# First stage of a two-layer decoder trunk: constants on another queue, the positions' product and the low parts in another order

## The chip, the cores and the metric

The kernel runs on one core of a Trainium2 chip. The metric is the device time of one launch, in microseconds (us): the median of three runs, and lower is better. A profile was taken of one execution; all rows below are of that execution, with times counted from the start of its span.

TensorE (PE in the rows; its weight loads are PEld) multiplies matrices, VectorE (DVE) and ScalarE (ACT) work element by element, GpSimd (POOL) does little here, and SyncE (SP) issues nearly all DMAs.

## What is computed

The reference is a decoder trunk of two layers over 256 tokens of width 1024. Each layer modulates its input by a conditioning vector, projects it, runs three kinds of attention side by side, and ends in a squared-ReLU MLP. What matters here is the very beginning, the modulation and the input projection of layer 0:

```python
mod = jax.nn.silu(c) @ ada_w[l] + ada_b[l]
sh_a, sc_a, g_a, sh_m, sc_m, g_m = [m_[:, None, :] for m_ in jnp.split(mod, 6, axis=-1)]
h = x * (1 + sc_a) + sh_a
parts = jnp.split(h @ w_in[l], SPLIT_POINTS, axis=-1)
...
ob, _ = banded_attention(rope(bq, positions), rope(bk, positions), bv, B_WINDOW - 1, sinks=sinks[l])
```

`rope` needs the sine and cosine of each position times a frequency.

## The kernel before

Every large product is done in three passes: each float32 operand is split into a high part and a low part, and the kernel adds high by high, high by low and low by high. A split is one ScalarE copy (`whi`, line 189) and one VectorE subtraction (`wlo`, line 191).

The first stage handles the 1024 input channels of layer 0 in eight chunks of 128. For each chunk `kc`:

- `first_h` computes the modulation of the chunk: sixteen small matmuls (line 177, `gv`) of the column form `crep` of silu(c) with a 1 MB block of the conditioning weights (`raw`, from `ada0`), a copy `rs` on ScalarE (line 324), two transposes of `x` (line 327) and a tiny product (line 328) that turns the sums into a column. VectorE adds the bias (`md`, line 330). Then ScalarE writes the high part of the modulated input (`hT`, line 332), VectorE computes the same in full (`h`, line 334) and subtracts to get the low part (`hT`, line 335).
- `first_load` loads the chunk's rows of the projection in two pieces (`w`, 768 and 792 columns, line 345), and `first_chunk` splits both pieces and multiplies: thirty matmuls `mm` of 256 columns (line 357 high by high, line 359 high weights by low input, line 360 low weights by high input) and six `mmv` of 280 columns (lines 402 to 404; 404 reads the low input). Lines 360 and 403 need the low parts of the weights, lines 359 and 404 the low part of `hT`.

The chunk's matmuls don't all stand together: a scheduler puts the end of chunk kc behind the `gv` matmuls and the column form of chunk kc+1, and the order on every engine is fixed when the program is built. `issue_after(X)` asks it to issue what is inside only once X has been issued.

All of this needs `p1`, one small tile (154 columns, 77 KB) that holds c, biases, a selector and the identity matrix. It is loaded by ScalarE's queue (line 138). SyncE's queue begins with the first `raw` block, the first half of `x`, the two pieces of `w`, and the next `raw`. TensorE starts with `WARM` matmuls of the identity by itself (`warm`, line 942), which compute nothing that is used, and has `FILL` more of them while the first `hT` is made.

The rotary tables are a generator, `rope_tables`, in three steps: a product of the positions' row by ones (line 661) with the multiplication by the frequencies (line 662); a chain of VectorE operations that brings the angles into range (lines 665 to 679); and two sines on ScalarE (lines 681 and 682), each of the switches of function costing a table load. `START` says after which chunk a step is taken: `o` is the next step of the tables, `r` the rows of the bias tables, `e` an exponential that switches ScalarE's table back.

Of the kernel before, what the change touches and what calls it, by code (L numbers as in the profile page):

```python
# [10 lines left out]
F32 = mybir.dt.float32  # L11
# [3 lines left out]
OP = mybir.AluOpType  # L15
# [12 lines left out]
SPARES = (('w', 'P', 'qk'), ('w', 'qk', 'P', 'mx'))  # L28
EARLY = 3
FO = (1, 3)  # L30
WARM = 8
TURN = 6
ORDER = ('kv0..21s4.3sa5.s.Acb.6.B7C..Ee', '.ts..q0412...ss3s.kva5cb.67AB.E..Ce')
GV = ('v', 'h', 'v', 'v', 'v')
START = ('', 'or', 'oe', '', '', '', '', '', 'cbbp')
FILL = 3
GROUPS = ((0, 4, 0), (4, 8, 32))


# [84 lines left out]
def trunk_kernel(ctx: ExitStack, tc: tile.TileContext, a):  # L124
    nc = tc.nc
# [9 lines left out]


    p1 = cst.tile([128, NP1], F32, name="p1")
    nc.scalar.dma_start(p1, a["p1"])
    pi32 = att.tile([128, S], I32, name="pi32", tag="pTc", bufs=2)
    nc.gpsimd.dma_start(pi32[0:1], bass.AP(tensor=a["positions"].tensor, offset=a["positions"].offset, ap=[[S, 1], [1, S]]))  # L140
    frs = cst.tile([128, 2], F32, name="frs")
# [165 lines left out]
                    fill.pop(0)  # L307


    SUMS, H32 = [], []  # L310

    def first_h(kc):

        gv = ps.tile([128, 512], F32, name="gv", tag="pt")
        tp = gv[:, 256:512].rearrange("p (b t) -> p b t", b=2)
        t = rawload(a["ada0"][kc])
        if kc % 2 == 0:
            nc.sync.dma_start(x[:, :, kc * 128:kc * 128 + 256], a["x"][:, :, kc * 128:kc * 128 + 256])
        for k in range(KC):
            for s in range(2):  # L320
                j = 2 * (k % 2) + s
                end = gemv_mm(gv, t, k, j, (k * 2 + s) * 128, 128, k < 2, k >= KC - 2)
        rs = u2("rs")
        SUMS.append(nc.scalar.activation(rs[:, :128], gv[:, :128], AF.Copy).ins)
        yield end.ins
        for b in range(2):
            nc.tensor.transpose(tp[:, b], x[:, b, kc * 128:kc * 128 + 128], ident)
        nc.tensor.matmul(gv[:, 128:130], rs[:, :128], p1[:, 24:26], start=True, stop=True)
        md = sm.tile([128, 2], F32, name="md0")
        nc.vector.tensor_tensor(md, gv[:, 128:130], p1[:, 8 + 2 * kc:10 + 2 * kc], op=OP.add)  # L330

        nc.scalar.activation(hT[:, 0, kc], gv[:, 256:512], AF.Identity, bias=md[:, 1:2], scale=md[:, 0:1])
        h32 = u2("h32")[:, :S]
        H32.append(nc.vector.tensor_scalar(h32, gv[:, 256:512], md[:, 0:1], md[:, 1:2], op0=OP.mult, op1=OP.add).ins)
        nc.vector.tensor_tensor(hT[:, 1, kc], h32, hT[:, 0, kc].bitcast(F32), op=OP.subtract)
        yield

    def first_load(kc):
# [9 lines left out]
    def first_chunk(kc, ts, prs, vs):  # L348

        with tc.issue_after(SUMS[kc]):  # L350
            ws = [parts(t, m, behind=H32[kc]) for t, m in ts]
        for pr, o in enumerate(prs):
            hi, lo = ws[pr // 3]
            for i in range(2):
                c = slice((2 * pr % 6 + i) * 128, (2 * pr % 6 + i + 1) * 128)

                nc.tensor.matmul(o[:, i], hi[:, c], hT[:, 0, kc], start=kc == 0 and i == 0, stop=False,
                                 skip_group_check=True)
                nc.tensor.matmul(o[:, i], hi[:, c], hT[:, 1, kc], start=False, stop=False, skip_group_check=True)
                nc.tensor.matmul(o[:, i], lo[:, c], hT[:, 0, kc], start=False, stop=kc == KC - 1,  # L360
                                 skip_group_check=True)
            yield
        hi, lo = (w[:, 512:] for w in ws[1])
        for b, o in enumerate(vs):
            v_mm(o, b, kc, hi, lo)
        yield
# [286 lines left out]
    def rope_tables(o):  # L653

        t = new_P()
        an, k, f, g = (t[:, i] for i in range(4))
        row = u2("row")[0:1]
        nc.vector.memset(row[:, S:S + 128], 1.0)
        with tc.issue_after(crep_set.ins):
            nc.vector.tensor_copy(row[:, :S], pi32[0:1])  # L660
        nc.tensor.matmul(o, row[:, S:S + 128], row[:, :S], start=True, stop=True)
        nc.vector.tensor_scalar(an, o, frs[:, 0:1], None, op0=OP.mult)
        yield
        magic = 1.5 * 2 ** 23
        nc.vector.tensor_scalar(k, an, 1.0 / (2 * math.pi), magic, op0=OP.mult, op1=OP.add)
        nc.vector.tensor_scalar(k, k, magic, None, op0=OP.subtract)
        c1 = 6.28125
        c2 = float(np.round((2 * math.pi - c1) * 2 ** 20) / 2 ** 20)
        c3 = 2 * math.pi - c1 - c2
        for c in (c1, c2, c3):  # L670
            nc.vector.scalar_tensor_tensor(an, k, -c, an, op0=OP.mult, op1=OP.add)

        nc.vector.scalar_tensor_tensor(f, an, -1.0, an, op0=OP.mult, op1=OP.max)
        nc.vector.tensor_scalar(f, f, -1.0, math.pi / 2, op0=OP.mult, op1=OP.add)

        nc.vector.tensor_scalar(k, an, -1.0, math.pi, op0=OP.mult, op1=OP.add)
        nc.vector.tensor_tensor(g, an, k, op=OP.min)
        nc.vector.tensor_scalar(k, an, -1.0, -math.pi, op0=OP.mult, op1=OP.add)
        nc.vector.tensor_tensor(g, g, k, op=OP.max)
        yield  # L680
        nc.scalar.activation(cosT, f, AF.Sin)
        nc.scalar.activation(sinT, g, AF.Sin)
        nc.vector.tensor_scalar(sinT, sinT, frs[:, 1:2], None, op0=OP.mult)
        yield
# [255 lines left out]
    def warm_up(n):  # L940
        for i in range(n):
            nc.tensor.matmul(warm[:, :128], ident, ident, start=True, stop=True)
# [7 lines left out]
    for kc in range(KC + 1):  # L950
        h = first_h(kc) if kc < KC else iter(())
        if kc == 0:
            end = next(h)
            with tc.issue_after(end):
                next(rt)
            w0, _ = first_load(0)
        if kc:
            ch = first_chunk(kc - 1, w0, prs, vs)
            end = next(h, None)
            if kc < KC:  # L960
                w0, loaded = first_load(kc)
            for _ in range(FO[1]):
                next(ch)
            if FO[0] and end:
                with tc.issue_after(end):
                    next(ch)
            next(h, None)
            next(h, None)
            for _ in ch:
                pass  # L970
        else:
            next(h)
            warm_up(FILL)
        for j in START[kc]:
            if j == "o":
                next(rt)
            elif j == "r":
                btab = bias_tables(bias_rows())
            elif j == "e":

                nc.scalar.activation(se[:, 0], sinT[:, 0:KC], AF.Exp)
            else:

                with tc.issue_after(loaded):
                    if j == "c":
                        nc.sync.dma_start(co, a["co"])
                    elif j == "p":
                        nc.sync.dma_start(p2, a["p2"])
                    else:
                        next(btab)  # L990
# [304 lines left out]
```

## Time and profile before

| | |
|---|---|
| median of 3 runs | 697.76 us (697.71 to 699.91) |
| the profiled execution's own time | 696.37 us |
| its span in the trace | 694.6 us |
| TensorE busy | 668.2 us, 96% of the span |
| VectorE busy | 497.6 us, 72% |
| ScalarE busy | 402.6 us, 58% |
| DMA moved | 167.55 MB, mean 241 GB/s |

The span leaves out 1.77 us of the execution's own time. An engine's busy time counts the union of its instructions; TensorE's instructions overlap, so a row's duration is longer than its distance to the next row.

### The profile page before, as it was taken

How to read it: one execution, taken by the hardware profiler on the slowest of the kernel's cores; microseconds unless marked ns; L12 is line 12 of the kernel's file. 1: busy time of each engine (PE TensorE's matmuls, PEld its weight loads, DVE VectorE, ACT ScalarE, POOL GpSimd, SP SyncE). 2: the span in 40 equal slices, each digit the busy share in tenths (PEclk: the TensorE clock that was granted, in tenths of full speed). 3: DMA queues.
4: the chain of work that ended last, by engine and by line, in shares of the span. 5: the costliest groups of instructions: out<-in, count | busy, mean ns of one | idle time of the engine just before them, and what ended most of it. 6: DMA issues, size and time to landing. Idle time of an engine off the chain costs nothing.

```text
span 694.6 us, 11202 instructions
## 1 busy us (share of the span) xinstructions
PE 668.2 (96%) x4302; PEld 550.1 (79%) x4302; DVE 497.6 (72%) x965; ACT 402.6 (58%) x792; POOL 43.1 (6%) x43
## 2 busy tenths in 40 slices
PE   5999999999999999999999999999999999999995
PEld 4888859558888888788889967867898888888884
DVE  3444968958798878888877967657679755555756
ACT  2534474874855555556746356688474655656641
POOL 0000200000400000000013010000130000000004
PEclk9999999999999999999999999999999999999998
DMA  8879788669359899889763958610438965655501
GB/s 324 290 270 351 263 325 277 236 232 345 127 223 365 311 371 341 326 334 341 278 242 122 347 175 309 238 62 1 182 137 290 377 220 189 210 188 186 182 0 62
DMA packets 29474, 167.55 MB, mean 241 GB/s; under 512 B 3247, under 2 KB 6475, under 8 KB 11884
## 3 DMA queue, kind: packets, MB, share of 16 engines
q1 hardware_dynamic: 29148, 166.73, 65.9%
q8 instruction: 34, 0.56, 0.3%
q14 instruction: 20, 0.16, 0.1%
q10 hardware_dynamic: 144, 0.08, 0.1%
q0 software_dynamic: 128, 0.02, 0.0%
HBM read 165.74 MB, written 1.08 MB: 240 GB/s over the span
## 4 chain that ended last, share of the span: by engine, by line
PE 87%; DVE 6%; ACT 4%; issue 1%; DMA 1%; POOL 0%; DVEq 0%; POOLq 0%
PE mm L394 14%; PE mmv L411 8%; PE m L1189 8%; PE m L1190 8%; PE m L1191 8%; PE mm L395 7%; PE s L734 3%; PE tp L702 2%; PE mm L383 2%; PE mm L381 2%; PE mm L382 2%; PE wo L1124 2%; PE wo L1126 2%; PE wo L1125 2%; PE gv L177 2%; PE acc L750 2%
## 5 line engine op out<-in xcount | busy, mean ns | idle before, releaser
L191 DVE TENSOR_TENSOR wlo<-raw,whi 128x1024 fp32r<-128x1024 f32 (+3 forms) x174 | 196.7, 1154 | 49.9 <-ACT whi L189 48.5
L189 ACT ACTIVATE whi<-raw 128x1024 fp32r<-128x1024 f32 (+3 forms) x183 | 178.8, 1003 | 34.9 <-PE mm L394 14.5
L394 PE MATMUL mm<-hT,whi 128*128 128x512 f32 x416 | 148.1, 399 | 0.0
L395 PE MATMUL mm<-hT,wlo 128*128 128x256 f32 x416 | 116.2, 281 | 1.2 <-DVE wlo L191 1.2
L1189 PE MATMUL m<-whi,mx 128*128 128x512 f32 x250 | 97.8, 391 | 0.0
L1190 PE MATMUL m<-wlo,mx 128*128 128x512 f32 x250 | 97.7, 391 | 0.0
L1191 PE MATMUL m<-whi,mx 128*128 128x512 f32 x250 | 97.2, 390 | 0.0
L394 PEld LDWEIGHTS mm<-hT,whi 128*128 128x128 f32 x416 | 78.1, 188 | 20.8 <-issue 2.1
L395 PEld LDWEIGHTS mm<-hT,wlo 128*128 128x128 f32 x416 | 78.5, 189 | 3.4 <-DVE wlo L191 2.3
L255 DVE SCALAR_TENSOR_TENSOR qk<-raw,se,qk 128x1024 f32<-128x1024 f32 x56 | 71.2, 1282 | 0.2
L397 ACT ACTIVATE P<-mm 128x256 f32<-128x256 f32 x52 | 19.7, 379 | 66.0 <-PE mm L395 66.0
L1189 PEld LDWEIGHTS m<-whi,mx 128*128 128x128 f32 x250 | 46.9, 188 | 10.1
L411 PE MATMUL mmv<-whi,hT 128*128 128x256 f32 (+2 forms) x352 | 53.9, 298 | 1.0 <-ACT hT L492 1.0
L1191 PEld LDWEIGHTS m<-whi,mx 128*128 128x128 f32 x250 | 46.9, 188 | 10.0
L1190 PEld LDWEIGHTS m<-wlo,mx 128*128 128x128 f32 x250 | 46.9, 188 | 8.9
L690 ACT ACTIVATE P<-P,sxt 128x128 f32<-128x128 f32 (+1 forms) x96 | 42.8, 448 | 18.2 <-DVE sxt L688 18.0
L411 PEld LDWEIGHTS mmv<-whi,hT 128*128 128x128 f32 x352 | 48.0, 189 | 2.5 <-ACT hT L492 1.5
L446 POOL TENSOR_TENSOR ve<-ve,co 128x1 f32<-128x1 f32 x8 | 4.4, 551 | 543.6 <-DVE ve L445 443.6
L381 PE MATMUL mm<-hT,whi 128*128 128x256 f32 x128 | 37.6, 294 | 0.0
L383 PE MATMUL mm<-hT,wlo 128*128 128x256 f32 x128 | 37.3, 291 | 0.1
L382 PE MATMUL mm<-hT,whi 128*128 128x256 f32 x128 | 36.6, 286 | 0.0
L398 DVE TENSOR_TENSOR P<-P,mm 128x256 f32<-128x256 f32 x52 | 21.7, 417 | 18.6 <-ACT P L397 18.5
(244 smaller groups left out, 1126.6 us busy)
## 6 DMA issues: line engine op xcount, KB each, us to landing
raw<-in_mlp_w_dram SPq DMA_DIRECT2D x64, 1024.0 KB, 6.0
raw<-in_ada_dram SPq DMA_DIRECT2D x32, 1024.0 KB, 5.4
raw<-in_adag_dram SPq DMA_DIRECT2D x16, 1024.0 KB, 6.2
raw<-in_w_in_dram SPq DMA_DIRECT2D x9, 1024.0 KB, 6.9
raw<-in_cmp_w_dram SPq DMA_DIRECT2D x8, 1024.0 KB, 6.8
raw<-in_w_out_dram SPq DMA_DIRECT2D x8, 1024.0 KB, 4.7
w<-in_w_in_dram SPq DMA_DIRECT2D x8, 396.0 KB, 7.2
w<-in_w_in_dram SPq DMA_DIRECT2D x8, 384.0 KB, 3.2
```

What stands on the lines that cost most here:

```text
L189: nc.scalar.activation(hi, t, AF.Copy)
L191: (eng or nc.vector).tensor_tensor(lo, t, hi.bitcast(F32), op=OP.subtract)
L255: nc.vector.scalar_tensor_tensor(ac, src, by, ac, op0=OP.mult, op1=OP.add)
L381: nc.tensor.matmul(o[:, i], hi[:, c], hT[:, 0, kc], start=kc == 0, stop=False, skip_group_check=True)
L382: nc.tensor.matmul(o[:, i], hi[:, c], hT[:, 1, kc], start=False, stop=False, skip_group_check=True)
L383: nc.tensor.matmul(o[:, i], lo[:, c], hT[:, 0, kc], start=False, stop=kc == KC - 1, skip_group_check=True)
L394: nc.tensor.matmul(o, hi[:, c], hT[:, :, kc], start=kc == 0, stop=False, skip_group_check=True)
L395: nc.tensor.matmul(o[:, 0], lo[:, c], hT[:, 0, kc], start=False, stop=kc == KC - 1, skip_group_check=True)
L411: nc.tensor.matmul(o, hT[:, x_, kc, t], ws[kc][w_], start=kc == 0 and x_ + w_ == 0, stop=kc == KC - 1 and w_ == 1)
L1189: nc.tensor.matmul(o, f[:, 0, i, t], hi, start=first, stop=False)
L1190: nc.tensor.matmul(o, f[:, 0, i, t], lo, start=False, stop=False)
L1191: nc.tensor.matmul(o, f[:, 1, i, t], hi, start=False, stop=lastk)
```

## The change

Five edits, all in the first stage:

- `p1` is loaded by SyncE's queue, ahead of everything else on it.
- `rope_tables` has one step more: the cast of the positions into a row stands by itself, and the product with the multiplication by the frequencies comes after VectorE's `md` of chunk 0. The range reduction moves from chunk 1 to chunk 2 and must follow that chunk's `h`; the sines and the exponential move from chunk 2 to chunk 3.
- The low parts of the weights of a chunk are issued after the low part of `hT` (`LOW`), no longer after the full `h` (`H32`).
- `WARM` goes from 8 to 9, `FILL` from 3 to 2.
- The row of the positions is no longer held back behind the last `gv` matmul of chunk 0.

```diff
-WARM = 8
+WARM = 9
...
-START = ('', 'or', 'oe', '', '', '', '', '', 'cbbp')
-FILL = 3
+START = ('', 'r', 'o', 'oe', '', '', '', '', 'cbbp')
+FILL = 2
...
-    nc.scalar.dma_start(p1, a["p1"])
+    nc.sync.dma_start(p1, a["p1"])
...
-        nc.vector.tensor_tensor(md, gv[:, 128:130], p1[:, 8 + 2 * kc:10 + 2 * kc], op=OP.add)
+        MD.append(nc.vector.tensor_tensor(md, gv[:, 128:130], p1[:, 8 + 2 * kc:10 + 2 * kc], op=OP.add).ins)
...
-        nc.vector.tensor_tensor(hT[:, 1, kc], h32, hT[:, 0, kc].bitcast(F32), op=OP.subtract)
+        LOW.append(nc.vector.tensor_tensor(hT[:, 1, kc], h32, hT[:, 0, kc].bitcast(F32), op=OP.subtract).ins)
...
-            ws = [parts(t, m, behind=H32[kc]) for t, m in ts]
+            ws = [parts(t, m, behind=LOW[kc]) for t, m in ts]
...
             nc.vector.tensor_copy(row[:, :S], pi32[0:1])
+        yield
         nc.tensor.matmul(o, row[:, S:S + 128], row[:, :S], start=True, stop=True)
...
-            end = next(h)
-            with tc.issue_after(end):
-                next(rt)
+            next(h)
+            next(rt)
...
             next(h)
+            with tc.issue_after(MD[0]):
+                next(rt)
             warm_up(FILL)
...
-                next(rt)
+                with tc.issue_after(H32[-1]):
+                    next(rt)
```

The orders differ in the first stage and shortly after it; from the first units of attention on they are the same on every engine. Three places matter.

TensorE at the start of the program, as a difference (`warm<-p_78` is the idle matmul, `warm<-row` the positions' product, `gv<-p_78,rs` the column form):

```order
-L942 MATMUL warm<-p_78 128x128 x8
+L943 MATMUL warm<-p_78 128x128 x9
 L177 MATMUL gv<-raw,crep 32x128 x16
 L327 MATMUL gv<-p_78,x 128x128 x2
-L661 MATMUL warm<-row 128x256
 L328 MATMUL gv<-p_78,rs 128x2
-L942 MATMUL warm<-p_78 128x128 x3
+L662 MATMUL warm<-row 128x256
+L943 MATMUL warm<-p_78 128x128 x2
 L357 MATMUL mm<-hT,whi 128x256 x2
```

The positions' product has moved behind the column form. Behind the last row there came two L402 and then L359 before; now there come two L359, one L402, and then L360.

VectorE in chunk 0, before (`P<-warm,frs` is the multiplication by the frequencies, the `P<-P` rows are the range reduction):

```order
L662 TENSOR_SCALAR P<-warm,frs 128x256
L330 TENSOR_TENSOR md_158<-gv,p_78 128x2
L665 TENSOR_SCALAR P<-P 128x256
L666 TENSOR_SCALAR P<-P 128x256
L671 SCALAR_TENSOR_TENSOR P<-P 128x256
L334 TENSOR_SCALAR h_161<-gv,md_158 128x256
L191 TENSOR_TENSOR wlo<-w_151,whi 128x768
L335 TENSOR_TENSOR hT<-h_161,hT 128x256
L191 TENSOR_TENSOR wlo<-w_153,whi 128x792
```

VectorE in chunk 0, after the change:

```order
L330 TENSOR_TENSOR md_157<-gv,p_78 128x2
L663 TENSOR_SCALAR P<-warm,frs 128x256
L334 TENSOR_SCALAR h_160<-gv,md_157 128x256
L335 TENSOR_TENSOR hT<-h_160,hT 128x256
L191 TENSOR_TENSOR wlo<-w_150,whi 128x768
L191 TENSOR_TENSOR wlo<-w_152,whi 128x792
```

The range reduction is gone from here, the frequencies stand behind `md`, and the low part of `hT` stands ahead of both low parts of the weights, as in every later chunk.

TensorE around the column form of chunk 2, before:

```order
L328 MATMUL gv<-p_78,rs 128x2
L359 MATMUL mm<-hT,whi 128x256
L360 MATMUL mm<-hT,wlo 128x256
L357 MATMUL mm<-hT,whi 128x256
L359 MATMUL mm<-hT,whi 128x256
L360 MATMUL mm<-hT,wlo 128x256
L403 MATMUL mmv<-wlo,hT 128x280
L404 MATMUL mmv<-whi,hT 128x280
L403 MATMUL mmv<-wlo,hT 128x280
L404 MATMUL mmv<-whi,hT 128x280
L357 MATMUL mm<-hT,whi 128x256 x4
L402 MATMUL mmv<-whi,hT 128x280 x2
```

TensorE at the same place after the change:

```order
L328 MATMUL gv<-p_78,rs 128x2
L403 MATMUL mmv<-wlo,hT 128x280
L404 MATMUL mmv<-whi,hT 128x280
L402 MATMUL mmv<-whi,hT 128x280
L403 MATMUL mmv<-wlo,hT 128x280
L404 MATMUL mmv<-whi,hT 128x280
L357 MATMUL mm<-hT,whi 128x256 x3
L359 MATMUL mm<-hT,whi 128x256 x3
L357 MATMUL mm<-hT,whi 128x256
L360 MATMUL mm<-hT,wlo 128x256
```

Four matmuls fewer of chunk 1 stand behind the column form, and chunk 2's own begin with three L357, three L359 and soon an L360; before, there came four L357 and two L402, and only then the first L359.

VectorE in the same chunk 2, after the change, has two operations of the range reduction between its own:

```order
L334 TENSOR_SCALAR h_324<-gv,md_321 128x256
L666 TENSOR_SCALAR P<-P 128x256
L335 TENSOR_TENSOR hT<-h_324,hT 128x256
L667 TENSOR_SCALAR P<-P 128x256
L191 TENSOR_TENSOR wlo<-w_282,whi 128x768
L672 SCALAR_TENSOR_TENSOR P<-P 128x256
L191 TENSOR_TENSOR wlo<-w_284,whi 128x792
```

L666 stands ahead of the low part of `hT`, L667 ahead of the first low part of the weights; before, nothing of the range reduction stood in chunk 2.

## Rows read from the trace of the kernel before

**Rows 1.** Whom TensorE waited for, whole span: us in total, times, longest.

```profile
PE warm L942 <- DMA p<-in_p_dram: 6.5, 1, 6.5
PE mm L359 <- DVE hT L335: 2.2, 5, 0.8
...
PE sw L920 <- ACT ct L915: 0.9, 1, 0.9
```

**Rows 2.** The chain that ended last, first 60 us: start, length, what.

```profile
0.74 5.72 DMA p<-in_p_dram
...
18.29 0.12 PE mm L359
```

**Rows 3.** Timeline, chunk 0: start, duration, engine, line, instruction, idle time before.

```profile
0.74 0.39 SPq L145 DMA_DIRECT2D raw<-in_ada_dram  x1
...
1.20 0.66 SPq L318 DMA_DIRECT2D x<-in_x_dram  x1
...
6.50 3.55 PE L942 MATMUL warm<-p 128*128 128x128 f32 x16 [6.50 <-DMA p<-in_p_dram]
...
9.98 1.08 PE L177 MATMUL gv<-raw,crep 128*32 128x128 f32 x32
...
11.83 0.69 PE L661 MATMUL warm<-row 1*128 1x256 f32 x2
...
12.46 0.38 PE L328 MATMUL gv<-p,rs 128*128 128x2 f32 x2
12.56 0.48 DVE L662 TENSOR_SCALAR P<-warm,frs 128x256 f32<-128x256 f32 x1 [4.63 <-PE warm L661]
12.96 0.15 DVE L330 TENSOR_TENSOR md<-gv,p 128x2 f32<-128x2 f32 x1
13.08 0.29 DVE L665 TENSOR_SCALAR P<-P 128x256 f32<-128x256 f32 x1
...
14.54 0.95 DVE L191 TENSOR_TENSOR wlo<-w,whi 128x768 fp32r<-128x768 f32 x1
15.40 0.42 DVE L335 TENSOR_TENSOR hT<-h,hT 128x256 fp32r<-128x256 f32 x1
...
15.87 0.39 PE L359 MATMUL mm<-hT,whi 128*128 128x256 f32 x1 [0.83 <-DVE hT L335]
...
19.07 1.28 ACT L681 ACT_TABLE_LOAD   x1
```

**Rows 4.** Timeline around the column form of chunk 2, in order of time.

```profile
27.10 0.28 PE L328 MATMUL gv<-p,rs 128*128 128x2 f32 x2
...
27.49 0.16 DVE L330 TENSOR_TENSOR md<-gv,p 128x2 f32<-128x2 f32 x1 [2.85 <-PE gv L328]
...
27.68 0.56 ACT L332 ACTIVATE hT<-gv,md 128x256 fp32r<-128x256 f32 x1 [0.72 <-DVE md L330]
...
28.28 0.55 DVE L334 TENSOR_SCALAR h<-gv,md 128x256 f32<-128x256 f32 x1 [0.63 <-ACT hT L332]
...
28.44 1.01 PE L357 MATMUL mm<-hT,whi 128*128 128x256 f32 x4
...
29.28 0.42 PE L402 MATMUL mmv<-whi,hT 128*128 128x280 f32 x2
...
30.08 0.39 PE L359 MATMUL mm<-hT,whi 128*128 128x256 f32 x1 [0.39 <-DVE hT L335]
```

**Rows 5.** Profile page, DMA issues: queue, count, KB each, median us to landing.

```profile
w<-in_w_in_dram SPq DMA_DIRECT2D x8, 384.0 KB, 3.2
```

**Rows 6.** Engines and DMA in two stretches; granted clock, DMA share, GB/s stand last.

```profile
2.00:3.00 1.00, 0.00 (x0) 0.00 (x0) 0.00 (x0) 0.45 (x1) 0.59 (x1) 1.00 0.42 95
3.00:4.00 1.00, 0.00 (x0) 0.00 (x0) 0.00 (x0) 0.00 (x0) 0.00 (x0) 1.00 0.99 386
```

**Rows 7.** Line 942, TensorE's idle matmuls: shortest, median, longest in ns.

```profile
L942 PE MATMUL warm<-p x22: 273/421/582, 6.5 to 13.8; 128*128 128x128 f32 x22
```

**Rows 8.** DMAs issued from 1.0 to 1.6 us: queue, KB, us to landing.

```profile
x<-in_x_dram SPq DMA_DIRECT2D x1, 256.0 KB, 5.9
```

More of the change, by code (lines that the diff above doesn't have):

```diff
@@ L307, in filler @@
                     fill.pop(0)
-    SUMS, H32 = [], []
+    SUMS, MD, H32, LOW = [], [], [], []
     def first_h(kc):
```

## The prediction, made before the changed kernel was run

> **What bounds the kernel now.** I read the page first: TensorE is busy for 96% of the span (the table above), so a change pays where it removes time in which TensorE stands still. The list of its waits shows how little that is: 6.5 us at the start, until `p1` has landed, and then waits of a few tenths [rows 1]. The chain that ended last begins with the load of `p1` and then runs through the first stage's matmuls, with no other DMA in it [rows 2]. The timeline of chunk 0 shows the pieces: TensorE starts at 6.50, the idle matmuls last until `gv` starts at 9.98, the positions' product holds the column form until 12.46, and the first product with a low `hT` starts at 15.87, after 0.83 of waiting [rows 3]. A later chunk shows the steady pattern: in chunk 2 TensorE waits 0.39 us for the low part of `hT` [rows 4]. From shortly behind the stage on all engines keep their order, so what the stage gains or loses is passed on to the end.
>
> **Step 1, `p1` ahead of everything.** It has 77 KB (128 x 154 x 4 bytes) and landed 5.72 us after its issue at 0.74, at 6.46 [rows 2], while the first `raw` (1 MB) and half of `x` were moved by the same DMA engines. In front of them it needs only its own time. From below: a 384 KB piece on SyncE's queue lands in 3.2 us [rows 5]; the 307 KB that `p1` has less take 0.8 us at 386 GB/s [rows 6]; that leaves 2.4 us, a landing at 3.1. From above: such a piece's whole 3.2, a landing at 3.9; farthest, no gain at all, 6.46. Between 2 and 3 us the DMA engines moved only 95 GB/s [rows 6], and this slow beginning now falls on `p1`; so I take 3.5, between the two near ends. Gain 2.96 us.
>
> The Trainium skill (DMA: Bandwidth & Descriptors, Issuing engines are not separate DMA queues) says that transfers started by different engines end up on the same DMA engines and interleave, and that issuing from several engines saves little more than issue time. Read as a rule on the choice of the queue, it would make this step worth nothing, and the sum below about 0 instead of 3 us. The trace agrees on the sharing: 77 KB took as long as the megabyte beside them. It stands behind the first rival below.
>
> **Step 2, nine idle matmuls.** Sixteen records (two to a matmul) take 9.98 - 6.50 = 3.48 us [rows 3], 0.22 each; the shortest last 273 ns where the median lasts 421 [rows 7], so two more cost between 2 x 0.07 (the mean less the difference) and 2 x 0.22; I take 0.25. `gv` could then start at 3.54 + 3.48 + 0.25 = 7.27. Is its data there? `x` stands right behind the first `raw` on the queue and landed at 1.20 + 5.9 = 7.1 [rows 3, 8]; its 256 KB take 0.7 at 386 GB/s [rows 6], so `raw` landed near 6.4. It is now issued 0.46 later (the distance of the queue's first two issues [rows 3]): 6.9, hidden by 0.4. `gv` gains 9.98 - 7.27 = 2.71 us.
>
> **Step 3, chunk 0 from `gv` to the continuous run.** The column form now starts where the product did, 0.63 earlier (11.83 instead of 12.46 [rows 3]), and `md` follows it by 0.39, as in chunk 2 [rows 4], instead of 0.50 behind the frequencies: together 0.74. Behind `md` VectorE has the frequencies. Their product starts about 0.25 after the column form, and its result reaches VectorE 0.73 later (11.83 to 12.56 [rows 3]): they start at `md` + 0.6 and hold VectorE for 0.4 (12.56 to 12.96). So `h` starts at `md` + 1.0, not + 0.79 as in chunk 2 [rows 4], the low `hT` at + 1.58, and TensorE's first L359 0.47 behind that (15.40 to 15.87 [rows 3]), at + 2.05; before it was + 2.91. But two L359 and one L402 further on, L360 needs the low weights, which now stand behind the low `hT`: about 0.4 and 0.95 later [rows 3], at `md` + 2.9. So the continuous run begins no sooner behind `md`; TensorE has only one matmul more done by then, five instead of four, 0.12 [rows 2]. Step 3: 0.74 + 0.12 = 0.86 us. The idle matmul that `FILL` loses lay in a wait, and so does its absence.
>
> **Step 4, the other chunks.** Before, chunks 2 to 4 each wait twice: 0.39 for the low `hT`, and four L357 take 0.84 where 4 x 0.12 would do [rows 2, 4], because the last of them needs the second `whi`: 0.36. With the 1.4 us of L359's waits outside chunk 0 [rows 1] that is 1.4 + 3 x 0.36 = 2.5 us. Now the low `hT` comes 0.87 sooner in each chunk, the low weights 0.4 later, and the order asks for them differently. In chunks 4 to 7 TensorE has twelve matmuls of the chunk before behind the column form (1.5 us), then three L357, and reaches L359 about 0.1 too early; L360 comes behind a `gv` (1.1 us) except in chunk 7, where it waits some 0.4: 0.8 us in all. In chunk 3 a table load of 1.28 us [rows 3] and a cosine stand ahead of ScalarE's high `hT` and delay it by about 0.4: with the waits behind it 0.5. Chunk 2 is the bad one. Only five matmuls stand behind its column form (0.65 us), so L357 waits 0.3 for the high `hT`, which ends 0.75 behind `md` [rows 4]; L359 waits 0.9 for the low `hT`, which L666 (0.29, like L665 [rows 3]) pushes back; and L360 waits 0.7 for the low weights, which L667 pushes back: 1.9 us. Chunk 1 costs 0.2. Sum 0.2 + 1.9 + 0.5 + 0.8 = 3.4 against 2.5: a loss of 0.9, with bounds of 0.2 (the tenths are within what such sums can tell) and 1.5. I take 0.6.
>
> Behind the stage TensorE waited 0.9 us at line 920 for ScalarE [rows 1]. That matmul now stands nine matmuls (1.1 us) earlier, and ScalarE's copy ahead of a split of 0.8 instead of behind it: 0, give or take 0.7.
>
> **Sum.** 2.71 + 0.86 - 0.6 = 2.97 us. The profiled execution's 696.37 would become 693.4; it lies 1.4 under the median of the runs, and the prediction is for the median: 697.76 - 3.0 = 694.8 us.
>
> **Rivals.**
>
> *`p1` comes no sooner.* The queue begins slowly whoever is first, and `p1` lands with the crowd. For it: the 95 GB/s until 3 us [rows 6], and that no small transfer at the head of that queue is seen. Against it: from 3 us on 386 GB/s were moved, nearly all of it not `p1`. Then the sum is 0.86 - 0.6 - 0.25 = 0, and the time 697.8 us.
>
> *The clock rises later.* The idle matmuls began at a pace that fits 1.2 GHz and ended at one that fits 2.4 GHz (421 and 273 ns [rows 7]); the rise fell into the burst. If it falls behind it, `gv` takes some 1.0 us more and each matmul after it 0.1. Where it comes with the tenth matmul of chunk 0, 2 us of the gain are gone: 696.8 us. The Trainium skill (TensorE: Matmul & The Clock Gate, What's actually happening) says that the watch on TensorE's activity runs freely and doesn't start afresh with a kernel, so that the place of the rise differs from run to run; one trace can't show it, and it would hold for the kernel before as well.
>
> *The low weights become the wait in every chunk.* This one ends on the other side. If chunks 3 to 7 fared like chunk 2, each waiting 1.9, they would lose 9.5 instead of the 1.3 that I counted: 8.2 us more, 703.0 us. It decides from a mean wait of 1.3 us in these five chunks on: 1.0 more than counted in each eats the 3 us and 2 more. Against it: only chunk 2 has range reduction between VectorE's own steps and so few matmuls behind its column form.
>
> **How the numbers follow.** The forecast gets 0.68, no sooner 0.13, the later clock 0.11, waits everywhere 0.08. About 0.3% (2.1 us) is what a measurement of this kernel can tell from no change. The forecast's own range is a gain of 1.9 to 4.4 (`p1` at 3.1 adds 0.4 before `raw` binds, at 4.4 it takes 0.9; step 4 and line 920 give or take 0.7 together): 693.4 to 695.9. The two mild rivals lie within 0.3% or just beside it, so the range reaches up towards them, and down to where all bounds meet: 692.8 to 697.2. Faster 0.68, same 0.23, slower 0.09.
>
> **What would show it.** Step 1: TensorE's first row at about 3.5, released by `p1`. Step 2: `gv` at 7.3, without a wait for `raw`. Step 3: `md` 2.24 behind the start of `gv` instead of 2.98, L359 2.0 behind `md`, L360 0.9 behind that. Step 4: waits of 0.3, 0.9 and 0.7 in chunk 2, tenths elsewhere, and line 360 as a new line among TensorE's waits. A first row after 5 us, idle matmuls that stay at 421 ns, or waits near 1 us in the chunks behind chunk 2 would make the prediction wrong.

## The result, and the profile after

The changed kernel takes 694.23 us (median of 5 runs, 692.37 to 694.73) where the kernel before took 697.76 beside it (697.2 to 700.3). The ratio is 0.9942, with a 95% interval of 0.9917 to 0.9966: faster by 3.5 us, where 3.0 were predicted. The profiled execution took 694.23 us, with a span of 692.5; the span before was 694.6, so from profile to profile the gain is 2.1 us, and the rest of the 3.5 lies in the other executions of the kernel before. Two executions far longer than the others (1306.82 us of the kernel before, 1653.25 us of the kernel "changed, filled" below, whose only profile that was) are left out of all that follows.

The chain that ended last begins with `p1` as before, but this piece is short (start, length, what):

```profile
0.74 1.89 DMA p<-in_p_dram
```

`p1` lands 1.89 us after its issue; it was 5.72 [rows 2]. The waits of TensorE over the whole span (us in total, times, longest) show what took the place of those in [rows 1]:

```profile
PE warm L943 <- DMA p<-in_p_dram: 2.7, 1, 2.7
...
PE mm L383 <- DVE wlo L191: 0.9, 1, 0.9
...
PE warm L943 <- DVE P L663: 0.6, 1, 0.6
...
PE mm L359 <- DVE hT L335: 0.5, 1, 0.5
...
PE sw L921 <- ACT ct L916: 0.3, 1, 0.3
PE mm L360 <- DVE wlo L191: 0.3, 1, 0.3
...
PE mm L357 <- ACT hT L332: 0.2, 1, 0.2
```

The start has lost 3.8 us of waiting, line 359 1.7 of its 2.2, and line 921 (920 before) 0.6. New are 0.9 at line 383, a product shortly behind the stage, and 0.3 at line 360; the wait at the idle matmuls of `FILL`, 0.6 here, was 0.26 at line 942 before. The timeline of chunk 0 answers to [rows 3] (start, duration, engine, line, instruction, idle time before):

```profile
2.67 4.21 PE L943 MATMUL warm<-p 128*128 128x128 f32 x18 [2.67 <-DMA p<-in_p_dram]
...
6.89 1.73 PE L177 MATMUL gv<-raw,crep 128*32 128x128 f32 x32
...
9.01 0.44 PE L327 MATMUL gv<-p,x 128*128 128x128 f32 x2 [0.40 <-ACT rs L324]
9.68 0.16 DVE L330 TENSOR_TENSOR md<-gv,p 128x2 f32<-128x2 f32 x1 [2.44 <-ACT whi L189]
...
10.77 0.71 PE L943 MATMUL warm<-p 128*128 128x128 f32 x4 [0.58 <-DVE P L663]
...
11.20 0.42 DVE L335 TENSOR_TENSOR hT<-h,hT 128x256 fp32r<-128x256 f32 x1
...
11.68 0.80 PE L359 MATMUL mm<-hT,whi 128*128 128x256 f32 x2
...
12.28 0.43 PE L402 MATMUL mmv<-whi,hT 128*128 128x280 f32 x1
...
12.55 0.58 PE L360 MATMUL mm<-hT,wlo 128*128 128x256 f32 x1
...
14.00 0.41 PE L359 MATMUL mm<-hT,whi 128*128 128x256 f32 x1
14.21 0.41 PE L360 MATMUL mm<-hT,wlo 128*128 128x256 f32 x1
...
15.02 1.10 PE L177 MATMUL gv<-raw,crep 128*32 128x128 f32 x32
```

Two things are to be seen. The first `gv` lasts 1.73 us, where it lasted 1.08 [rows 3] and the second one lasts 1.10. And L359 and L360 at 14.00 and 14.21 last 0.41 each and stand 0.21 apart. In the kernel before, two such matmuls lasted 0.28 and stood 0.12 apart:

```profile
18.25 0.28 PE L360 MATMUL mm<-hT,wlo 128*128 128x256 f32 x1
18.37 0.28 PE L357 MATMUL mm<-hT,whi 128*128 128x256 f32 x1
```

The windows of the changed kernel show the clock of the second stretch (a row has the stretch, its length, the busy time and count of TensorE, its weight loads, VectorE, ScalarE and GpSimd, and then the granted clock, the DMA share and GB/s):

```profile
10.00:11.00 1.00, 0.42 (x3) 0.23 (x3) 0.77 (x2) 1.00 (x2) 0.00 (x0) 1.00 0.97 410
11.00:12.00 1.00, 1.00 (x7) 0.83 (x7) 0.96 (x3) 0.19 (x1) 0.00 (x0) 0.85 0.97 396
12.00:13.00 1.00, 1.00 (x5) 0.85 (x5) 1.00 (x2) 0.00 (x0) 0.00 (x0) 0.50 1.04 418
...
14.00:15.00 1.00, 1.00 (x5) 0.76 (x4) 0.00 (x0) 0.00 (x0) 0.00 (x0) 0.50 0.89 279
15.00:16.00 1.00, 1.00 (x33) 0.83 (x32) 0.00 (x0) 0.00 (x0) 0.00 (x0) 0.95 1.03 426
```

The granted clock falls near 11.7 to 0.50 (1.2 of 2.4 GHz) and is back shortly after 15. In the kernel before it stood at 1.00 through the whole stage of the profiled execution. What TensorE did ahead of the fall: it stood still for 0.40 at line 327, waiting for ScalarE's copy, and for 0.58 at line 943, waiting for VectorE. Standing still isn't enough by itself, though: in the profile of the kernel before, TensorE was busy for only 0.17 of the microsecond from 15 to 16, and the clock stayed up:

```profile
15.00:16.00 1.00, 0.17 (x2) 0.13 (x2) 1.00 (x3) 0.00 (x0) 0.00 (x0) 1.00 0.92 359
```

Chunk 2, as in [rows 4]:

```profile
25.32 0.28 PE L328 MATMUL gv<-p,rs 128*128 128x2 f32 x2
...
25.71 0.16 DVE L330 TENSOR_TENSOR md<-gv,p 128x2 f32<-128x2 f32 x1 [3.50 <-PE gv L328]
...
26.06 0.29 PE L404 MATMUL mmv<-whi,hT 128*128 128x280 f32 x1
...
26.53 0.62 PE L357 MATMUL mm<-hT,whi 128*128 128x256 f32 x3 [0.17 <-ACT hT L332]
...
27.64 0.62 PE L359 MATMUL mm<-hT,whi 128*128 128x256 f32 x3 [0.50 <-DVE hT L335]
...
28.71 0.38 PE L360 MATMUL mm<-hT,wlo 128*128 128x256 f32 x1 [0.33 <-DVE wlo L191]
```

It waits at the three places that the prediction named. By the distances of the starts (one matmul takes 0.12, three 0.36, four 0.48) the waits come to 0.35, 0.75 and 0.59, 1.7 us in all, where 1.9 were forecast.

### The profile page after: what moved, and what is told of

Same layout as the page of the kernel before. It is cut to its first block, busy times and chain, and to the rows that moved or that the text cites. A ratio compares the mean times of both kernels' runs of the same rounds, so it can differ in the third digit from the quotient of the medians.

```text
span 692.5 us, 11203 instructions
## 1 busy us (share of the span) xinstructions
PE 670.9 (97%) x4302; PEld 552.6 (80%) x4302; DVE 498.9 (72%) x965; ACT 402.1 (58%) x792; POOL 43.3 (6%) x43
## 3 DMA queue, kind: packets, MB, share of 16 engines
HBM read 165.74 MB, written 1.08 MB: 241 GB/s over the span
## 4 chain that ended last, share of the span: by engine, by line
PE 89%; DVE 6%; ACT 3%; issue 1%; DMA 0%; POOL 0%; DVEq 0%; POOLq 0%
PE mm L394 14%; PE mmv L411 8%; PE m L1192 8%; PE m L1193 8%; PE m L1194 8%; PE mm L395 7%; PE s L735 3%; PE tp L703 2%; PE mm L381 2%; PE mm L383 2%; PE gv L177 2%; PE mm L382 2%; PE wo L1127 2%; PE wo L1129 2%; PE wo L1128 2%; PE acc L751 2%
## 5 line engine op out<-in xcount | busy, mean ns | idle before, releaser
L397 ACT ACTIVATE P<-mm 128x256 f32<-128x256 f32 x52 | 19.7, 379 | 66.0 <-PE mm L395 65.9
L691 ACT ACTIVATE P<-P,sxt 128x128 f32<-128x128 f32 (+1 forms) x96 | 42.8, 448 | 19.9 <-DVE sxt L689 19.7
L689 DVE CUSTOM_DVE_ANT_0 P<-s,bias 128x128 f32<-128x128 f32 (+1 forms) x80 | 26.0, 350 | 15.7 <-PE s L735 13.3
```

## The experiments

Two marks in a profile divide the time: `md` of chunk 0, and `KK`, ScalarE's first copy of a product that the whole stage has added up (line 1053 before, 1056 after), which stands at the stage's end. In the kernel before and in the changed one it reads:

```profile
64.69 0.60 ACT L1053 ACTIVATE KK<-mm 128x512 f32<-128x512 f32 x1 [2.58 <-PE mm L360]
62.17 0.60 ACT L1056 ACTIVATE KK<-mm 128x512 f32<-128x512 f32 x1 [2.45 <-PE mm L360]
```

The result of a run also gives its granted clock over the span, and with a few exceptions this sorts the runs. Where a profile shows no fall in the first stage it is 0.996 to 0.998 (seven of the other kernels and the one before); where it shows one, 0.994 or less (changed, changed with `WARM` 8, `p1` alone, low parts alone, no `FILL`). The kernels of the experiments were timed in four groups, each with runs of the kernel before beside it. In these its runs at 0.995 or more have medians of 696.68 to 697.15, so half a microsecond between kernels of different groups can't be told.

| kernel | median, us (range, runs) | ratio to before, 95% interval | runs at 0.995 or more: number, median | `md` 0 | `md` 0 to `KK` |
|---|---|---|---|---|---|
| before, beside the experiments | 697.05 to 698.14 (medians of four groups) | | 42 of 75, 696.94 | 12.96 | 51.73 |
| changed | 694.23 (692.37 to 694.73, 5) | 0.9942 [0.9917, 0.9966] | 1 of 5, 692.37 | 9.68 | 52.49 |
| `p1` alone | 693.6 (693.0 to 697.0, 12) | 0.9942 [0.9923, 0.9962] | 9 of 12, 693.45 | 9.29 | 53.26 |
| all but `p1` | 697.25 (695.09 to 698.46, 12) | 0.9985 [0.9969, 1.0001] | 3 of 12, 695.94 | 11.34 | 51.38 |
| low parts alone | 702.02 (697.63 to 704.21, 12) | 1.0038 [1.0016, 1.0061] | 4 of 12, 698.48 | 12.79 | 53.35 |
| `p1`, low parts, `WARM` | 697.88 (694.97 to 699.31, 12) | 0.9993 [0.9972, 1.0014] | 6 of 12, 695.46 | 9.66 | 51.83 |
| `p1` alone, no `FILL` | 695.77 (694.42 to 697.0, 12) | 0.9974 [0.9961, 0.9986] | 1 of 12, 697.0 | 10.38 | 54.07 |
| changed, filled | 693.24 (692.68 to 693.54, 5) | 0.9934 [0.9918, 0.9950] | 5 of 5, 693.24 | | |
| changed, filled, `WARM` 8 | 692.70 (692.37 to 693.63, 6) | 0.9931 [0.9916, 0.9946] | 6 of 6, 692.70 | 9.50 | 51.38 |
| changed, `WARM` 8 | 694.15 (692.24 to 694.97, 6) | 0.9946 [0.9928, 0.9963] | 1 of 6, 692.24 | 9.54 | 52.71 |
| changed, filled, ones | 692.63 (692.34 to 692.89, 6) | 0.9919 [0.9894, 0.9943] | 6 of 6, 692.63 | 8.99 | 51.35 |
| `p1` alone, filled | 693.67 (693.28 to 694.42, 7) | 0.9931 [0.9907, 0.9956] | 7 of 7, 693.67 | 9.55 | 51.66 |
| changed without the low parts | 693.21 (691.89 to 693.62, 6) | 0.9924 [0.9898, 0.9949] | 1 of 6, 691.89 | 8.70 | 51.14 |
| all that pays | 691.74 (691.51 to 692.43, 6) | 0.9905 [0.9888, 0.9922] | 6 of 6, 691.74 | 8.84 | 51.57 |

### `p1` alone

```diff
-    nc.scalar.dma_start(p1, a["p1"])
+    nc.sync.dma_start(p1, a["p1"])
```

> Theory (the early p1 carries the gain): the kernel before with p1 alone moved to SyncE's queue has its first TensorE row near 2.7 and gains 2.0 to 3.0 us, 694.8 to 695.8 us, ratio 0.996 to 0.997. First rival (the order carries the gain, because raw's landing and a slower clock eat what p1 gives): 697.3 to 697.8 us, ratio 0.999 to 1.000. Second rival (the gain needs both, since without the later product of the positions TensorE only waits longer for the row): first TensorE row near 2.7, but the column form of chunk 0 ends near 12 as before, 697 us.

693.6 us: `p1` carries the gain, as the theory had it, and more than it said, 1.2 us below its lower bound of 694.8. The ratio is that of the whole change. The edit touches this one DMA, and TensorE's matmuls come in the order of before, so nothing else can have given it. The timeline of this kernel's chunk 0:

```profile
2.69 3.42 PE L942 MATMUL warm<-p 128*128 128x128 f32 x16 [2.69 <-DMA p<-in_p_dram]
6.33 1.08 PE L177 MATMUL gv<-raw,crep 128*32 128x128 f32 x32 [0.21 <-DMA raw<-in_ada_dram]
...
13.84 1.94 PE L177 MATMUL gv<-raw,crep 128*32 128x128 f32 x32
```

`gv` waits 0.21 for `raw` and starts at 6.33: a still earlier start of TensorE can't bring this `gv` forward. The second `gv` is the slow one here: the granted clock was low from 12.4 to 15.8.

### All but `p1`

```diff
-    nc.sync.dma_start(p1, a["p1"])
+    nc.scalar.dma_start(p1, a["p1"])
```

This is the changed kernel with `p1` back.

> Theory (the early p1 carries the gain): the changed kernel with p1 back on ScalarE's queue starts TensorE near 6.5 and keeps only what the order gives, 0.3 us less than before (0.86 of step 3 less 0.6 of step 4): 697.0 to 697.8 us, ratio 0.999 to 1.000. Rival (the order carries the gain): 694.3 to 695.3 us, ratio near 0.995. In both, its idle matmuls and column form lie in time as in the kernel before, so a clock that has risen by the column form would show a column form of 1.1 us and not 1.73.

697.25 us, a ratio whose interval reaches just past 1: the theory. Its profile has the changed kernel's order with a clock that stays up (`gv` takes 1.08, as the text expected of a clock that has risen):

```profile
9.19 1.08 PE L177 MATMUL gv<-raw,crep 128*32 128x128 f32 x32
11.34 0.16 DVE L330 TENSOR_TENSOR md<-gv,p 128x2 f32<-128x2 f32 x1 [4.37 <-ACT whi L189]
62.72 0.60 ACT L1056 ACTIVATE KK<-mm 128x512 f32<-128x512 f32 x1 [2.46 <-PE mm L360]
```

So it gives the order's own worth in the stage, 1.2 us: `md` stands 2.15 behind the start of `gv`, where it stood 2.98 behind it (0.83), and from `md` to `KK` it takes 51.38 us, where the kernel before took 51.73 (0.35). The same order took 52.49 from `md` to `KK` in the changed kernel's profile; the two differ there in the fall of the clock, which so cost 1.1 us.

### The low parts alone, and with `p1`

```diff
-        nc.vector.tensor_tensor(hT[:, 1, kc], h32, hT[:, 0, kc].bitcast(F32), op=OP.subtract)
+        LOW.append(nc.vector.tensor_tensor(hT[:, 1, kc], h32, hT[:, 0, kc].bitcast(F32), op=OP.subtract).ins)
...
-            ws = [parts(t, m, behind=H32[kc]) for t, m in ts]
+            ws = [parts(t, m, behind=LOW[kc]) for t, m in ts]
```

> The kernel before with the low parts of the weights behind the low part of hT, nothing else. Theory: in chunk 0 L359 starts 0.9 us sooner behind md, but L360 is late, so the run of matmuls begins as before; the other chunks win at L359 and lose at L360: 697.3 to 698.3 us, ratio 0.999 to 1.001. Rival (each chunk waits for its low weights as chunk 2 was expected to, near 1.9 us): above 700 us, ratio over 1.003. Rival (this edit carries the gain, through the late chunks that come 0.7 us sooner each): 694 to 695.5 us, ratio near 0.996.

The second kernel has this edit, `p1` on SyncE's queue, and `WARM` at 9.

> The changed kernel with the positions' product, the range reduction and the sines where they were before. Theory: md of chunk 0 comes 0.6 to 0.8 us later than in the changed kernel, chunk 2 is spared some 1 us of waits, and the time is within 0.7 us of the changed kernel's: 694.0 to 695.0 us, ratio 0.995 to 0.996. Rival (the positions' place carries the gain): 696.5 to 697.5 us, ratio above 0.998.

702.02 us and 697.88: both some 4 us above the kernel without the edit, where nothing and 0.7 were expected. The second is even above the range of its rival (696.5 to 697.5): once the low parts are moved, taking the positions' steps back costs all that `p1` gave. 702.02 is what the rival of the low weights foresaw, but not by its mechanism: line 360 waits 0.2 us in the whole span of either kernel, and in the second kernel, whose profile shows no fall, the stage takes 51.83 us, as before. The time is lost behind the stage: from `KK` to the end of the span it takes 632.1 us there, against 630.3 in the changed kernel and 629.9 to 630.9 in the kernel before and in those with `p1` alone. The waits of TensorE in that stretch of the second kernel (64 to 200 us) have lines that the kernel before doesn't have at that size:

```profile
PE tp L702 <- DVE P L696: 0.9, 2, 0.6
...
PE tp L780 <- DVE PC L778: 0.7, 1, 0.7
PE s L798 <- DVE sxt L688: 0.7, 1, 0.7
PE cv L899 <- DVE sxt L688: 0.6, 1, 0.6
```

With the low parts moved and the positions' steps where they were, the scheduler writes another order of the softmax and its matmuls behind the stage; with all five edits it doesn't. Besides, eight and six of the twelve runs of these two kernels have a granted clock of 0.992 or less, and in the first one's profile it is down twice, from 16.3 to 19.7 and again between 114 and 120. The runs at 0.995 or more put the order's share at 1.5 to 2.0 us (698.48 less 696.94, 695.46 less 693.45); how much of the rest the falls make was not tried apart.

### Without the idle matmuls of `FILL`

```diff
-FILL = 3
+FILL = 0
```

This is the kernel with `p1` alone, less three matmuls that compute nothing and lie in a wait.

> The kernel before with p1 on SyncE's queue, and without the three idle matmuls of FILL (work that computes nothing and lies in a wait). Theory (idle stretches in chunk 0 make the clock fall): the fall near 12 us comes in most runs, median 695 to 697 us against 693.6 with them. Rival (FILL's matmuls have no effect on the clock): 693.6 us as with them, two thirds of the runs at 693.0 to 693.8.

695.77 us: leaving out idle work makes the kernel 2.2 us slower, as the theory had it, and no run stays at 693. Windows of this kernel's profile, with the granted clock third from the end:

```profile
10.00:11.00 1.00, 0.26 (x2) 0.17 (x2) 0.97 (x4) 0.43 (x1) 0.00 (x0) 1.00 0.98 412
11.00:12.00 1.00, 0.56 (x3) 0.36 (x3) 0.96 (x4) 0.89 (x2) 0.00 (x0) 0.88 0.94 383
12.00:13.00 1.00, 0.77 (x2) 0.44 (x2) 1.00 (x3) 0.00 (x0) 0.00 (x0) 0.50 1.05 421
...
18.00:19.00 1.00, 1.00 (x8) 1.00 (x8) 0.00 (x0) 0.98 (x2) 0.00 (x0) 0.71 1.06 416
```

TensorE is busy for 0.26 and 0.56 of the two microseconds in front of the fall, and this fall lasts until 18.6. The stage takes 54.07 us, 0.8 more than with the three (53.26, with the shorter fall) and 2.3 more than without a fall (51.73). The first `gv` of this profile also ran slowly (1.93 us), and it stands ahead of `FILL`; so the comparison rests on the runs (11 of 12 under 0.995, where it was 3 of 12), not on this pair of profiles. One run, at 697.0, has a granted clock of 0.997; what made it slow stays open.

### The stretch filled

```diff
+            end = next(h)
+            with tc.issue_after(end):
+                warm_up(1, prs[4][:, 0, :128])
...
-            warm_up(FILL)
+            with tc.issue_after(MD[0]):
+                warm_up(5, prs[4][:, 0, :128])
```

The changed kernel's idle matmuls of chunk 0 write another tile, so that they needn't wait for line 663, and there are six instead of two. The three kernels here are this one, this one with `WARM` at 8, and the changed kernel with `WARM` at 8 alone.

> The changed kernel with the two idle matmuls of FILL replaced by six that wait for nothing on VectorE: two behind the first gv, four behind the positions' product. Theory (TensorE stands still for about 1 us between the first column form and chunk 0's matmuls, after which the granted clock falls to 0.5 for some 3.4 us, which costs 1.7 to 2 us): the granted clock stays at 1.00 from 9 to 20 us, the median falls to 692.0 to 692.8 us, near the changed kernel's one run of 692.37, and the 12 runs lie within 1 us. Rival (the fall has nothing to do with what TensorE does there): as the changed kernel, 694.2 us, with a fall near 12 us in the profile. Second rival (the idle matmuls hold up chunk 0): above 694.5 us, with L357 later than 2.0 us behind md.

> As the kernel with six idle matmuls in chunk 0, with 8 ahead of the first gv instead of 9. Theory (raw has landed by 6.33, so the ninth idle matmul holds up the first gv): gv starts near 6.4 instead of 6.9 and the time falls by 0.3 to 0.5 us more, 691.6 to 692.4 us. Rival (fewer idle matmuls leave the clock low for longer): the first gv still at the slow pace, 1.7 us or more, and no gain or a loss of up to 1 us.

> The changed kernel with 8 idle matmuls at the start instead of 9, nothing else. Theory (raw has landed by 6.33): the first gv starts near 6.4, 693.6 to 694.0 us. Rival (raw lands at 6.9, as the prediction had it): gv starts at 6.9 after a wait of 0.4 for raw, 694.2 us.

693.24, 692.70 and 694.15 us. The filled kernels do what the theory says where it matters: all eleven runs have a granted clock of 0.996 or 0.997 and lie within 0.9 and 1.3 us, while the unfilled one with `WARM` 8 has a fall in five of six runs, as the changed kernel in four of five. The first filled kernel gains only 1.0 us on the changed one, not 1.4 to 2.2, and the second one is 0.3 above its theory's range. The second one's timeline and windows:

```profile
6.41 1.94 PE L177 MATMUL gv<-raw,crep 128*32 128x128 f32 x32
...
9.94 1.16 PE L943 MATMUL mm<-p 128*128 128x128 f32 x8
```

```profile
11.00:12.00 1.00, 0.83 (x6) 0.55 (x5) 0.98 (x2) 0.01 (x1) 0.00 (x0) 1.00 0.96 392
12.00:13.00 1.00, 0.74 (x7) 0.63 (x6) 1.00 (x2) 0.00 (x0) 0.00 (x0) 1.00 1.02 412
```

The clock stays at 1.00 where it fell, and the stage takes 51.38 us. But the first `gv` takes 1.94 us. The number of idle matmuls ahead doesn't decide that: behind eight it took 1.08 with `p1` alone, and behind nine it took 1.73 in the changed kernel and 1.08 in the one without the low parts. It starts at 6.41 without a wait for `raw`, so it could start 0.5 sooner, and ends 0.3 sooner. `WARM` 8 or 9 alone makes no difference that these runs can tell (694.15 and 694.23); `gv` starts at 6.55 there, without a wait for `raw`, as its theory had it, but the time is the rival's.

### Idle matmuls that don't wait for `p1`

```diff
-WARM = 8
+WARM = 13
...
+    ones_w = cst.tile([128, 128], F32, name="onesw")
+    nc.vector.memset(ones_w, 1.0)
...
-            nc.tensor.matmul(to, ident, ident, start=True, stop=True)
+            nc.tensor.matmul(to, ones_w, ones_w, start=True, stop=True)
```

> The changed kernel with six idle matmuls in chunk 0 that wait for nothing on VectorE, and all idle matmuls on a tile of ones written by VectorE at the start of the program, 13 ahead of the first gv, so that they don't wait for p1. Theory (the first gv runs at half pace because the idle matmuls begin only at 2.7 us): TensorE starts before 2 us, the first gv runs near 6.4 us at 1.1 us instead of 1.9, and the median is 691.4 to 692.2 us, 0.6 to 0.9 under the kernel with 8 idle matmuls on p1. Rival (the clock rises no sooner): gv at 1.9 us, 692.5 to 693.2 us.

```profile
1.28 5.61 PE L945 MATMUL warm<-onesw 128*128 128x128 f32 x26 [1.28 <-DVE onesw L941]
6.81 1.08 PE L177 MATMUL gv<-raw,crep 128*32 128x128 f32 x32
```

The timeline is the theory's: TensorE starts at 1.28, and the first `gv` runs at full pace. That the early start did it isn't shown, since `gv` also took 1.08 in four profiles with a start near 2.7 (`p1` alone, the same filled, with low parts and `WARM`, and changed without the low parts). Thirteen may be too many: `gv` starts at 6.81, and `raw` let it go at 6.33 with `p1` alone and at 6.54 with `p1` alone, filled. `md` comes at 8.99 and not 9.50. The median doesn't follow: 692.63 against 692.70, which is what the rival foresaw of the time, though not of `gv`. Only the spread is smaller (0.55 us for 1.3).

### The order at an equal clock

`p1` alone, with idle matmuls that wait for nothing on VectorE (two behind `gv`, three in `FILL`):

```diff
             with tc.issue_after(end):
+                warm_up(1, prs[4][:, 0, :128])
                 next(rt)
...
-            warm_up(FILL)
+            with tc.issue_after(SUMS[0]):
+                warm_up(4, prs[4][:, 0, :128])
```

> The kernel before with p1 on SyncE's queue, and with two idle matmuls behind the first gv and three in FILL that wait for nothing on VectorE; the positions' product and the low parts stand as in the kernel before. Theory (the order is worth some 1 us at an equal clock, and p1 alone and the changed kernel differ so little in their medians because the clock falls more often in the changed one): runs between 693.0 and 694.2 us, median 693.4, 0.5 to 1.0 above the changed kernel with 8 and 6 idle matmuls (692.70). Rival (the order is worth nothing): median 692.4 to 692.9.

And the changed kernel with the low parts back:

```diff
-            ws = [parts(t, m, behind=LOW[kc]) for t, m in ts]
+            ws = [parts(t, m, behind=H32[kc]) for t, m in ts]
```

> The changed kernel with the low parts of the weights behind the full h again, so p1, the positions' steps, WARM and FILL are changed and the low parts are not. By the prediction's step 3 the column form gains 0.74 and L359 waits longer; by step 4 the later chunks wait for the low hT as before: md of chunk 7 at 57 to 58 us as in the changed kernel or up to 0.9 sooner. Theory (the low parts' edit is worth nothing by itself): 693.7 to 695.0 us. Rival (the low parts' edit carries what the order gives): 695.5 to 696.5 us, with the late chunks' md 7.0 apart instead of 6.3.

693.67 us: with falls gone from both, the old order is 1.0 us slower than the new one (692.70, or 692.63 in the same group), as the theory had it. (The ratios of 0.9931 are equal because the kernel before had more falls beside this one, in 6 of 12 runs for 6 of 17.) 693.21 us: without the low parts' edit the changed kernel is 1.0 us faster, 0.5 below its theory's range, although five of its six runs have a fall. So the low parts' edit carries nothing beside the positions' edit, and what the order gives comes from the positions. The `md` of its last four chunks stand 6.2, 5.8 and 6.2 us apart, not 7.0 as the rival had it, and the last of them stands at 55.75, where 56.1 to 58 was expected.

### All that pays, together

`p1` first, the positions behind the column form, the low parts as before, twelve idle matmuls on ones, and the stretch filled as above.

> What the runs point to, together: p1 first on SyncE's queue, the positions' product behind the column form, the low parts of the weights behind the full h as in the kernel before, twelve idle matmuls on a tile of ones ahead of the first gv, and six that wait for nothing on VectorE in chunk 0. Theory (the low parts' edit costs what the order gives in the late chunks, the clock's fall is gone, and gv runs at full pace): granted clock 1.00 from 6 to 20 us, all runs within 1 us, median 691.0 to 691.9 us. Rival (the low parts' edit pays once the clock stays up): 692.6 us or more, as the kernel with ones and the low parts' edit.

```profile
1.28 5.46 PE L945 MATMUL warm<-onesw 128*128 128x128 f32 x24 [1.28 <-DVE onesw L941]
6.66 1.08 PE L177 MATMUL gv<-raw,crep 128*32 128x128 f32 x32
```

691.74 us, 0.9905 of the kernel before, with all runs between 691.5 and 692.4: the fastest of all, and 2.5 us under the changed kernel. It is 0.9 under the kernel with ones and the low parts' edit, as the theory had it; that one had one idle matmul more and was timed in another group.

## Why the prediction was right

The time was right, and for its main reason, too: `p1`'s earlier landing carries the change. Its terms were less good than its sum, and that they come out near the measured gain is in part luck. In the two profiles `gv` gains 3.09 (2.71 forecast), `md` then 0.19 (0.74), the stage from `md` on loses 0.76 and what stands behind it 0.4, together 2.1 and not 2.97. The median gained 3.5, because the median execution of the kernel before was slower by 1.4 us than its profiled one.

**Step 1** was right in kind and too small: `p1` landed at 2.63, not 3.5, and below even the near bound of 3.1. The gain was 3.8 us, not 2.96. The estimate took the 384 KB piece's 3.2 us less 0.8 for the bytes; a small transfer that nothing is in front of took 1.89. (The Trainium skill, DMA: Bandwidth & Descriptors, Anatomy of one DMA — SWDGE (gpsimd) path, fits 2.0 us and the bytes at 436 GB/s to DMAs of GpSimd's path, by which an estimate for 77 KB would be 2.2 us; the row, on SyncE's queue, is somewhat below it.) The rule that a transfer's issuing engine matters little (the Trainium skill, DMA: Bandwidth & Descriptors, Issuing engines are not separate DMA queues) is not refuted by that. `p1` is issued at 0.74 in both kernels; the move changed its queue and put the first `raw` 0.46 behind it, and no run here tells these apart. What the row refutes is the first rival, that `p1` lands with the crowd.

**Step 2** gave back half of what step 1 won beyond its forecast. Nine idle matmuls took 4.21 us, not 3.73, since all of them ran at the slow pace (0.47 each). The prediction had named this as a sign of being wrong; the time held because `p1` had landed 0.87 sooner than forecast. `raw`, which was to hide behind them until 6.9, had landed by 6.33 with `p1` alone, where `gv` waited for it; here it made no difference. `gv` started at 6.89 and gained 3.09 us, not 2.71.

**Step 3**: `md` came 2.79 us behind `gv`'s start, not 2.24, because `gv` itself took 0.65 longer at the slow pace; without that it would be 2.14. The order's rows were right: L359 came 2.00 behind `md` (2.05 forecast) and L360 0.87 behind it (0.9).

**Step 4** failed as a term: a loss of 0.6 was taken, and the stage from `md` on gained 0.35 at an even clock (51.38 for 51.73), of which step 3 had 0.12. Chunk 2's waits are there, 1.7 us for the 1.9 forecast; the other chunks lack the waits that were given to them, 1.5 us together: lines 357, 359 and 360 have 1.0 in the list of waits, all of it in chunk 2. Behind the stage the low parts' edit brings a wait at line 383 (0.9), which the step didn't look at; line 921, where it said 0 give or take 0.7, gives 0.6 back. (In the two kernels with the positions' edit and without this one, line 383 has no wait, and line 921 has its 0.9 again.)

**The rival of the clock** came true in part, beside the forecast. It priced a late rise at 2 us of the gain. In the profile the first `gv` takes 0.65 more, and the clock then falls again in chunk 0, which the rival did not foresee; the fall costs 1.1. The rival set this against a kernel before whose clock stays up, as the one trace had it. But 33 of the 75 runs of the kernel before beside the experiments have a granted clock under 0.995, and their median is 699.81 where that of the others is 696.94. So both kernels pay for falls, the changed one more often (4 of 5 runs) but less each time (692.37 to 694.26). At an even clock the change is worth 4.6 us by its single run, and the prediction's 2.97 was too small. Why the changed kernel falls more often, by the idle matmul that `FILL` lost or by the wait of 0.58 that its others got, was not tried apart.

The rule that it quoted (the Trainium skill, TensorE: Matmul & The Clock Gate, What's actually happening), that the watch on TensorE isn't in step with the kernel, agrees with the traces: `p1` alone and the changed kernel with `WARM` 8 both start eight idle matmuls at 2.7, and the first `gv` takes 1.08 in one (at 6.33) and 1.93 in the other (at 6.55).

**The rival of the low weights** did not come: with all five edits line 360 waits once, 0.3 us, in chunk 2.

What stays open: why the filled kernels without and with ones differ by 0.5 us in the profile's `md` and not in the median; why the same `gv` runs slowly in some executions and not in others; and where the low parts' edit costs the 1.0 that the medians of whole kernels show. In the stage it costs 0.24 by one pair of profiles (51.38 and 51.14) and gains 0.22 by another (51.35 with it, 51.57 in the last kernel), and of the waits behind the stage 0.3 is left (0.9 less 0.6).

## What to carry to other kernels

Of five edits made together, the move of `p1` gave 3.5 us by itself at an even clock (693.45 for 696.94). The positions' later product gave nearly two more (691.74 for 693.67, both filled, the first with ones), and the low parts' edit took about one back. Time each alone, and sort the runs by the granted clock before judging tenths. A small transfer that everything waits for belongs in front of the large ones. Idle matmuls are worth something where TensorE would stand still in front of dense work: with those of `FILL`, which wait for VectorE, 9 of 12 runs with `p1` alone were at 0.995 or more, without them 1 of 12, and with those that wait for nothing on VectorE all 30 runs of five kernels.

## What the hardware showed unasked

The granted clock fell in the middle of a stage, not only at the start: in chunk 0 of the changed kernel, after TensorE had stood still for about 1 us in two pieces, it went from 1.00 to 0.50 and came back while TensorE was busy without a gap. Three unused matmuls (0.94 us) decided between 693.6 and 695.8 us. And the granted clock reads 1.00 from the start of the span, while the first nine idle matmuls take 0.47 each and the two of `FILL` later only 0.36; in the first 8 us the pace of the rows tells the clock, not that number. The landing of `p1` on ScalarE's queue also varied by itself: 6.46 in one profile [rows 2], 5.49 in another of the same queue (all but `p1`).
